# A Strassen MLP whose norms move into the output projection, with a PSUM bank of its own for each product and no elementwise work on GpSimd

## The chip, the cores and the metric

The kernel runs on one core of a Trainium2 chip. The metric is the device time of one execution in microseconds (us). Five engines work side by side, each through its own queue in order: TensorE (PE, matmuls and transposes), VectorE (DVE), ScalarE (ACT), GpSimd (POOL) and SyncE (SP), whose queue issues nearly all DMA transfers. Matmul results land in PSUM, which has eight banks of 512 fp32 values per partition; everything else on the chip lies in SBUF.

## The reference

One residual layer over x of 1024 tokens by 1024 channels, in fp32. An attention and pooling mixer (two branches, gated and merged) ends in an output projection, and an MLP follows:

```
merged = gates_pool * (y_pool @ w_branch_pool) + gates_attn * (y_attn @ w_branch_attn)
x  = x + merged @ w_out                       # output projection, residual
h2 = rmsnorm(x, g_ffn)                        # over the 1024 channels of a token
x  = x + square(relu(h2 @ w_up)) @ w_down     # w_up 1024 x 4096, w_down 4096 x 1024
```

## The kernel before

**Three matmuls for one.** To keep fp32 accuracy each operand is split into a high part (an ACT cast to the rounded type, line 109) and a low part (operand minus high part, line 110, on DVE or POOL). `mm3` (lines 115 to 117) issues high x high, high x low and low x high into the same bank. A split is therefore one ACT and one DVE or POOL instruction per operand tile.

**The stages.** Attention, pooling and gates come first, then the branch projections (`ba`) and the output projection: `out_proj` writes bank `op`, one half of the channels (`dh`) of one block of 128 tokens (t = 0 to 7) at a time, with 24 matmuls each. DVE adds the residual (line 813) and the row goes to DRAM (`yd`). The order is token half th and channel half dh: (0,0), (0,1), (1,1), (1,0), so tokens 0 to 3 are complete half-way and token 7 at the very end.

**The norms.** `norm_token` loads each token block back from DRAM (`yt`), squares and sums on ACT, takes the power -0.5 on POOL (line 235), scales on DVE (line 891, tile `hn`), and transposes on PE into the banks `hb` (line 895).

**The Strassen products.** Both MLP matmuls use the seven-product scheme of Strassen (in Winograd's form), once. The tokens' side of the up projection needs the quarters B11, B21 (tokens 0 to 3), B22 and the combinations T1 to T4 (tokens 0 to 3 with 4 to 7), each split in high and low. Products 1 and 2 need only B11 and B21. A pair p (0 to 15) is 256 columns of w_up: `up_pair` loads them (`wu`), makes the sums S1 to S4 (tiles `s`), splits them (`A`, `AS`), and runs seven products of 12 matmuls. Product 1 goes to bank X, product 2 to Y; 6 and 7 add to X, product 5 and then product 3 go to Z, product 4 to W. `finish` adds a saved partial result (DVE, line 855), applies relu (ACT, line 968) and squares (POOL, line 969). The results and four combinations of them (tiles `us`, DVE) go to DRAM as the operands of the down projection, which runs its seven products (banks DX, DY, DZ, DV) in 8 steps q of 24 matmuls, each with a 0.5 MB load of `ur`, one or two of `wd`, two splits (`u` and `w`) and mostly one difference (T).

**What sets the order.** The program is written in order, with the first part of pair p+1 (products 1 and 2) before the rest of pair p, and the scheduler of the framework sorts each engine's queue by its own time estimates, with the written order as priority. From then on each engine works its queue strictly in that order. Tiles come from pools with a number of buffers; a new tile waits until its buffer's last reader is done. The eight banks of PSUM go round: `bank(name)` takes the next.

## Time and profile before

| | us |
|---|---|
| median of 3 runs (lowest, highest) | 1636.32 (1632.89, 1637.15) |
| profiled execution: its time | 1636.88 |
| profiled execution: span, first to last instruction | 1635.1 |
| busy PE / DVE / ACT / POOL | 1557.7 / 966.0 / 766.2 / 736.6 |
| first matmul of the output projection | 842.2 |
| its last matmul starts | 929.05 |
| first up product starts | 974.08 |
| last down product's last matmul starts | 1631.08 |

PE counts as busy from a matmul's start to its modelled end, so a stage with PE at 100% has matmuls at full spacing. "Granted clock" is the share of full speed that the clock control gave to PE. In a row of groups stand busy us, the mean ns of one, then the idle time of the engine just before these instructions and what ended it.

### The profile page before, as it was taken

What the parts mean: (1) busy time and instruction counts of PE and PEld (TensorE: products, weight loads), DVE (VectorE), ACT (ScalarE), POOL (GpSimd) and SP (SyncE); (2) the same over time, 40 slices, a digit from 0 to 9 for tenths busy, and PEclk for the clock granted to TensorE, in tenths of its full rate; (3) what the DMA queues carried; (4) which work ended last, traced back from release to release, by engine and by line L of the source; (5) the groups of instructions that cost most, each with busy time, mean ns of one, the idle gap of its engine ahead of it and who ended that gap; (6) DMA issues with size and microseconds to landing.
All of it is one profiled execution on the core that took longest, in us unless ns stands there. A gap on an engine that the chain in (4) does not pass through costs nothing.

```text
span 1635.1 us, 22296 instructions
## 1 busy us (share of the span) xinstructions
PE 1557.7 (95%) x7649; PEld 1334.0 (82%) x7649; DVE 966.0 (59%) x2089; ACT 766.2 (47%) x1712; POOL 736.6 (45%) x691
## 2 busy tenths in 40 slices
PE   7999999999999999999999748999999999899999
PEld 6999999999999898887888636887777778688887
DVE  6776767777878787552321176655555474534453
ACT  6656565656665556544311164444434433333332
POOL 5424242425252523125532149876666554345443
PEclk9999999999999999999999959999999999999999
DMA  7112121202021212376342234444333378736763
GB/s 218 59 43 68 37 78 34 72 22 85 31 76 35 78 46 69 107 258 204 120 167 103 89 117 140 144 135 142 135 142 142 142 265 294 244 118 203 271 210 105
DMA packets 147707, 206.43 MB, mean 126 GB/s; under 512 B 9781, under 2 KB 86282, under 8 KB 147594
## 3 DMA queue, kind: packets, MB, share of 16 engines
q1 hardware_dynamic: 137098, 190.29, 35.0%
q10 hardware_dynamic: 10496, 14.72, 2.5%
q8 instruction: 60, 0.98, 0.3%
q14 instruction: 53, 0.43, 0.1%
HBM read 152.51 MB, written 52.46 MB: 125 GB/s over the span
## 4 chain that ended last, share of the span: by engine, by line
PE 80%; DVE 8%; DMA 5%; POOL 3%; issue 2%; ACT 2%; SPq 0%; ACTq 0%; POOLq 0%; DVEq 0%
PE z L117 5%; PE z L115 5%; PE z L116 5%; PE g L115 3%; PE g L116 3%; PE g L117 3%; PE DX L117 3%; PE DX L116 3%; PE DX L115 2%; PE X L115 2%; PE sc L485 2%; PE sc L486 2%; PE X L116 2%; PE X L117 2%; PE Z L115 2%
## 5 line engine op out<-in xcount | busy, mean ns | idle before, releaser
L115 PE MATMUL z<-wqkv,hT 128*128 128x384 f32 x512 | 175.0, 342 | 0.3 <-DVE qn L427 0.2
L117 PE MATMUL z<-wqkv,hT 128*128 128x384 f32 x512 | 174.6, 341 | 0.5 <-DVE hT L110 0.5
L116 PE MATMUL z<-wqkv,hT 128*128 128x384 f32 x512 | 174.1, 340 | 0.0
L235 POOL TENSOR_TENSOR ms<-ms,mhalf 128x4 f32<-128x4 f32 x64 | 66.6, 1041 | 159.1 <-DVE ms L234 140.0
L496 ACT ACTIVATE s<-s,nm 128x256 f32<-128x256 f32 (+7 forms) x128 | 99.6, 778 | 49.4 <-DVE nm L488 45.8
L116 PE MATMUL g<-hT,fwgate 128*128 128x512 f32 x256 | 101.0, 394 | 0.0
L117 PE MATMUL g<-hT,fwgate 128*128 128x512 f32 x256 | 101.0, 394 | 0.0
L115 PE MATMUL g<-hT,fwgate 128*128 128x512 f32 x256 | 100.9, 395 | 0.0
L115 PEld LDWEIGHTS z<-wqkv,hT 128*128 128x128 f32 x512 | 96.9, 189 | 4.2 <-DVE qn L427 0.8
L117 PEld LDWEIGHTS z<-wqkv,hT 128*128 128x128 f32 x512 | 96.9, 189 | 3.2 <-DVE hT L110 1.3
L116 PEld LDWEIGHTS z<-wqkv,hT 128*128 128x128 f32 x512 | 97.0, 189 | 3.0
L433 POOL TENSOR_TENSOR qn<-qn,ggh 128x128 f32<-128x128 f32 x64 | 32.4, 507 | 137.6 <-DVE qn L427 131.4
L969 POOL TENSOR_TENSOR u<-u 128x512 f32<-128x512 f32 x64 | 72.9, 1139 | 43.1 <-ACT u L968 43.1
L488 DVE CUSTOM_DVE_ANT_0 s<-sc,dist 128x512 f32<-128x512 f32 (+3 forms) x128 | 74.7, 586 | 22.3 <-PE sc L486 20.7
L110 POOL TENSOR_TENSOR wqkv<-rqkv,wqkv 128x384 fp32r<-128x384 f32 x60 | 63.3, 1073 | 20.0 <-ACT wqkv L109 18.2
L968 ACT ACTIVATE u<-u 128x512 f32<-128x512 f32 x64 | 40.4, 632 | 65.4 <-DVE u L855 65.0
L110 POOL TENSOR_TENSOR fwgate<-frgate,fwgate 128x512 fp32r<-128x512 f32 x32 | 45.0, 1408 | 53.3 <-ACT fwgate L109 53.2
L485 PE MATMUL sc<-K,Q 128*128 128x512 f32 (+2 forms) x192 | 67.4, 356 | 0.1
L486 PE MATMUL sc<-K,Q 128*128 128x512 f32 (+2 forms) x192 | 66.6, 354 | 0.0
L109 ACT CAST AS<-s 128x512 fp32r<-128x512 f32 x64 | 39.5, 620 | 55.6 <-PE X L117 19.9
L110 DVE TENSOR_TENSOR AS<-s,AS 128x512 fp32r<-128x512 f32 x32 | 37.1, 1160 | 45.4 <-ACT AS L109 45.1
L459 ACT CAST Q<-tk 64x128 fp32r<-64x128 f32 x128 | 33.3, 260 | 58.4 <-DVE Q L458 56.5
(525 smaller groups left out, 4903.9 us busy)
## 6 DMA issues: line engine op xcount, KB each, us to landing
wd<-in_w_down_dram SPq DMA_DIRECT2D x64, 512.0 KB, 4.5
wu<-in_w_up_dram SPq DMA_DIRECT2D x32, 512.0 KB, 3.8
udS<-us SPq DMA_DIRECT2D x64, 256.0 KB, 2.1
ur<-udS SPq DMA_DIRECT2D x32, 512.0 KB, 4.0
rqkv<-in_w_in_dram SPq DMA_DIRECT2D x64, 192.0 KB, 2.8
ud<-u SPq DMA_DIRECT2D x48, 256.0 KB, 2.5
ur<-ud SPq DMA_DIRECT2D x24, 512.0 KB, 4.3
frgate<-in_w_gate_dram SPq DMA_DIRECT2D x32, 256.0 KB, 2.7
```

The source lines that it names most:

```text
L109: nc.scalar.copy(hi, src)
L110: (lo_eng or nc.vector).tensor_tensor(lo, src, f(hi), op=ALU.subtract)
L115: nc.tensor.matmul(ps, lhs_hi, rhs_hi, start=first, stop=False, **kw)
L116: nc.tensor.matmul(ps, lhs_hi, rhs_lo, start=False, stop=False, **kw)
L117: nc.tensor.matmul(ps, lhs_lo, rhs_hi, start=False, stop=last, **kw)
L235: nc.gpsimd.tensor_tensor(dst, dst, mhalf[:, :n], op=ALU.pow)
L485: nc.tensor.matmul(dst, Q[:, i, 0, :], rhs, start=True, stop=False)
L486: nc.tensor.matmul(dst, Q[:, i, 1, :], rhs, start=False, stop=True)
L488: nc.vector.tensor_tensor_reduce(out=s[i][:, c : c + w], in0=sc[:, 0:w], in1=dist[:, o0 + c : o0 + c + w], scale=2.0 ** -(h + 1), scalar=B ...
L496: nc.scalar.activation(s[i][:, 0:n], s[i][:, 0:n], AF.Exp, bias=last, scale=-1.0, accum_out=Z[:, i, t : t + 1])
L968: nc.scalar.activation(r, r, AF.Relu)
L969: pool.tensor_tensor(r, r, r, op=ALU.mult)
```

## The change

The projection's norms, the pools of the MLP, the engines of the elementwise work and the order of the first pairs are rewritten. What is computed and the number of matmuls and transposes stay the same.

- **Norms inside the projection.** A token block stays in SBUF (`py`, four buffers) instead of being loaded back. `first_half` normalises tokens 0 to 3 behind the (1,1) blocks of the projection and writes what the combinations need of them to DRAM (`nd`); `second_half` normalises tokens 4 to 7 with the priority of the (1,0) blocks and makes T1, T2; `combine` makes T3, B22 and T4 later. ACT now scales by the root (a Copy with a scale), DVE multiplies by the gain, once for each half.
- **Four pairs ahead.** Products 1 and 2 of pairs 0 to 3 are written before the rest of pair 0; the second half of a pair's columns (A21, A22) is loaded later, by a transfer of its own. After that it is again one pair ahead.
- **Banks.** X has four banks, Y two, Z and W one each, by name. In the down projection there are two groups of four.
- **No elementwise work on POOL.** Low splits and S sums go to DVE, the squares to ACT. POOL keeps the power in the norms and the splits of `w_out`.
- **Other.** Weights and activations of the down projection get buffers of their own, its first three steps' operands are made early, and the difference T1 (`t1_made`) is made two steps behind. The finished quarters are stored through ACT's queue.

Up to the projection's (1,1) blocks the order of PE is the same instruction for instruction.

PE between the projection and product 6 of pair 0, before (`op` is the projection, `hb` the transposes of token blocks 0 to 7, the first digit behind X, Y or Z the pair; first matmul of each group):

```order
L117 MATMUL op7_0_10140<-wo10_6_1_10056,mT7_1_9620 128x512
L895 MATMUL hb0_0_10202<-identf_81,hn0_10195 128x128 x4
L895 MATMUL hb7_1_10464<-identf_81,hn7_10451 128x128 x4
L115 MATMUL X0_10551<-B11h_10215,A11_0_10553 128x512
L115 MATMUL Y0_10552<-B21h_10223,A12_0_10570 128x512
L115 MATMUL X1_10594<-B11h_10215,A11_1_10596 128x512
L115 MATMUL Y1_10595<-B21h_10223,A12_1_10613 128x512
L115 MATMUL X0_10551<-BT2h_10342,AS2_0_10639 128x512
```

and now, from the last matmul of the projection:

```order
L119 MATMUL op7_0_10292<-wo10_6_1_10204,mT7_1_9626 128x512
L117 MATMUL X0_10533<-B11h_9644,A11_0_10535 128x512
L117 MATMUL Y0_10534<-B21h_9646,A12_0_10552 128x512
L117 MATMUL X1_10598<-B11h_9644,A11_1_10600 128x512
L888 MATMUL hb5_0_10452<-identf_87,y5_10001 128x128 x4
L117 MATMUL X3_10696<-B11h_9644,A11_3_10698 128x512
L888 MATMUL hb7_1_10518<-identf_87,y7_10117 128x128 x4
L117 MATMUL Y2_10648<-B21h_9646,A12_2_10666 128x512
L117 MATMUL Y3_10697<-B21h_9646,A12_3_10715 128x512
L117 MATMUL X0_10533<-BT2h_10345,AS2_0_10751 128x512
L117 MATMUL Z0_10768<-BT1h_10347,AS1_0_10769 128x512
L119 MATMUL X0_10533<-BT2h_10345,AS2_0_10751 128x512
```

All 64 transposes stood alone behind the projection. Now the first 40 stand inside it, and the last 24 between the eight products (96 matmuls) that need only B11 and B21.

DVE in the same place now, from the add that completes token block 7 (entry 1 of this count) to the low halves of S2 and S1 of pair 0 (entries 55 and 56); shown are entries 1, 5, 10, 29, 36, 43, 49, 50, 51, 55 and 56:

```order
L823 TENSOR_TENSOR y7_10117<-op7_0_10292,y7_10117 128x512
L826 TENSOR_TENSOR t1_4_10411<-hb4_0_10422,t1_4_10411 128x512
L884 TENSOR_TENSOR y7_10117<-y7_10117,gfb_9648 128x512 x2
L826 TENSOR_TENSOR t1_7_10501<-hb7_0_10512,t1_7_10501 128x512
L112 TENSOR_TENSOR BT2l_10346<-t2_7_10502,BT2h_10345 128x4x128
L826 TENSOR_TENSOR t4_7_10593<-t4_7_10593,y7_10117 128x512
L823 TENSOR_TENSOR u11_3_10730<-Y3_10697,x1_3_10713 128x512
L823 TENSOR_TENSOR s1_0_10745<-wu0_1_10743 128x512
L826 TENSOR_TENSOR s2_0_10746<-s1_0_10745,wu0_0_10531 128x512
L112 TENSOR_TENSOR AS2_0_10751<-s2_0_10746,AS2_0_10751 128x512
L112 TENSOR_TENSOR AS1_0_10769<-s1_0_10745,AS1_0_10769 128x512
```

Before, this work was shared by DVE and POOL; now it is one queue, and all combinations of tokens 4 to 7 stand ahead of the first S sum.

PE in the steady state, before (first matmul of each product; the products in this order are 3, 4, 1, 2, 5):

```order
L115 MATMUL Z6_11616<-B22h_10355,AS4_6_11658 128x512
L115 MATMUL W7_11846<-BT4h_10361,A22_7_11847 128x512
L115 MATMUL X9_11874<-B11h_10215,A11_9_11876 128x512
L115 MATMUL Y9_11875<-B21h_10223,A12_9_11893 128x512
L115 MATMUL Z8_11936<-BT1h_10346,AS1_8_11937 128x512
```

and now (the last matmul of product 3 of pair 7, then the beginnings of what follows):

```order
L119 MATMUL Z7_11808<-B22h_10351,AS4_7_11850 128x512
L119 MATMUL X8_11744<-BT2h_10345,AS2_8_11951 128x512
L117 MATMUL X11_12224<-B11h_9644,A11_11_12226 128x512
L117 MATMUL Y10_12065<-B21h_9646,A12_10_12083 128x512
L117 MATMUL Z8_11968<-BT1h_10347,AS1_8_11969 128x512
L117 MATMUL W8_12038<-BT4h_10353,A22_8_12039 128x512
```

Between the end of product 3 of a pair and product 5 of the next, which now use the same bank, stand 18 matmuls: the last four of X8, twelve of X11 and two of Y10.

The diff, cut to what the prediction speaks of:

```diff
-N_OP, N_RW, N_SM, N_EV = 8, 8, 4, 9
+N_OP, N_E1, N_E2, N_R1, N_R2 = 8, 11, 6, 4, 3
...
+    nb_pool = pool_of(hs, "nb", 4, side="right")
+    pr1 = pool_of(hs, "pr1", N_R1, side="right")
+    py = pool_of(norms, "py", 4, side="right")
...
     def out_proj(ws, t, dh):
...
+        if t not in y:
+            y[t] = py.tile([P, D], F32, tag="y", name=f"y{t}")
+        nc.sync.dma_start(y[t][:, cs], x[t * P : (t + 1) * P, cs])
...
+    def norm_token(t, bank_fn):
...
+        nc.scalar.activation(sq, yn, AF.Square, accum_out=ss)
+        rsq(rs, ss, 1, 1.0 / D)
+        nc.scalar.activation(yn, yn, AF.Copy, scale=rs)
+        ps = []
+        for j in range(2):
+            js = slice(j * 512, (j + 1) * 512)
+            nc.vector.tensor_tensor(yn[:, js], yn[:, js], gfb[:, js], op=ALU.mult)
+            b = bank_fn(j, f"hb{t}_{j}")
...
+    def first_half(t):
+        b11, b21 = norm_token(t, lambda j, name: bank(name))
+        b_split("11", t * P, b11, dve)
+        b_split("21", t * P, b21, dve)
...
+        nc.sync.dma_start(nd[0, t], r11)
+        nc.sync.dma_start(nd[1, t], d21)
...
             out_proj(ws, t, dh)
+            if (th, dh) == (1, 1):
+                first_half(t - 4)
+            prio[t] = tc.cur_priority
...
+    bm = pool_of(mlp_ps, "bm", 1, PSUM)
+    bx = pool_of(mlp_ps, "bx", 1, PSUM)
...
+    def second_half(t):
+        c0 = (t - 4) * P
+        t1, t2 = (ev(f"{n}_{t}", (P, 4, P)) for n in ("t1", "t2"))
+        nc.sync.dma_start(t1, nd[0, t - 4])
+        b12, b22 = norm_token(t, lambda j, name: bm.tile([P, 512], F32, tag="ZW"[j], name=name))
+        sub(dve, t1, b12, t1)
+        sub(dve, t2, b22, t1)
...
+        b_split("T2", c0, t2, dve)
+        b_split("T1", c0, t1, dve)
...
-        X, Y = bank(f"X{p}"), bank(f"Y{p}")
+        A = load(0, pr1)
+        X = bx.tile([P, 512], F32, tag="X", name=f"X{p}", bufs=4)
+        Y = (bm if p % 2 else bx).tile([P, 512], F32, tag="Y", name=f"Y{p}")
...
-            pool.tensor_tensor(r, r, r, op=ALU.mult)
+            nc.scalar.activation(r, r, AF.Square)
...
-        add(pool, S1, A["21"], A["22"])
-        sub(pool, S2, S1, A["11"])
+        add(dve, S1, A["21"], A["22"])
+        sub(dve, S2, S1, A["11"])
...
-        Z = bank(f"Z{p}")
-        u_product(Z, "5", a_op(p, "S1", S1, pool))
+        Z = bm.tile([P, 512], F32, tag="Z", name=f"Z{p}")
+        u_product(Z, "5", a_op(p, "S1", S1, dve))
...
+    AHEAD = 4
+    for p, q in zip(range(AHEAD), ("T3", "22", "T4", "")):
+        next(pairs[p])
...
+        if q:
+            combine(q)
...
+    pur = pool_of(ctx, "pur", 3, side="right")
+    puo = pool_of(ctx, "puo", 8, side="right")
+    prw = pool_of(ctx, "prw", 7, side="right")
+    pwo = pool_of(ctx, "pwo", 8)
...
-        for n, src, eng in (("u", ur, dve), ("w", second(j, q), pool)):
-            hi, lo = (op([P, 2, 512], f"{n}{j}_{q}{x}") for x in "hl")
-            split(hi, lo, src, eng)
+        for n, src, pool_ in (("u", ur, puo), ("w", second(j, q), pwo)):
+            hi, lo = (pool_.tile([P, 2, 512], F32R, tag="op", name=f"{n}{j}_{q}{x}") for x in "hl")
+            split(hi, lo, src, dve)
...
+    def d_product(banks, j, last=False, early={}):
         for q in range(NQ - 2 if last else NQ):
-            d_step(banks, j, q, operands(j, q), range(4))
+            d_step(banks, j, q, early.get(q) or operands(j, q), range(4))
+            if j == "1" and q > 1:
+                t1_made(q - 2)
...
+    early = {q: operands("1", q) for q in range(3)}
```

More of the change, by code (lines that the diff above doesn't have):

```diff
@@ L773, in encoder_kernel @@
     ws_bp = load_cols2(w_branch_pool, 0, "bp0")
-    ypT = [load_split(p_dram, g * P, f"ypT{g}", htile) for g in range(4)]
+    ypT = [load_split(p_dram, g * P, f"ypT{g}", ypt_tile) for g in range(4)]
     mp, yT = [], []
@@ L820, in w_out_half, with b_split @@
         return ws
+    def b_split(q, c0, src, eng):
+        hi, lo = Bq[q]
+        split(hi[:, :, c0 : c0 + P], lo[:, :, c0 : c0 + P], src, eng)
+    def norm_token(t, bank_fn):
+        ss = const.tile([P, 1], F32, tag="nss", name=f"nss{t}", bufs=2)
+        rs = const.tile([P, 1], F32, tag="nrs", name=f"nrs{t}", bufs=2)
+        sq = nt.tile([P, D], F32, tag="sq", name=f"nsq{t}")
+        yn = y[t]
+        nc.scalar.activation(sq, yn, AF.Square, accum_out=ss)
[6 more added lines that the diff above has]
+            b = bank_fn(j, f"hb{t}_{j}")
+            for i in range(4):
+                k = 4 * j + i
+                nc.tensor.transpose(b[:, i * P : (i + 1) * P], yn[:, k * P : (k + 1) * P], identf)
+            ps.append(b.rearrange("p (a b) -> p a b", a=4))
+        return ps
+    nd = dram.tile([2, 4, P, 4, P], F32, name="nd")
+    def first_half(t):
+        b11, b21 = norm_token(t, lambda j, name: bank(name))
+        b_split("11", t * P, b11, dve)
+        b_split("21", t * P, b21, dve)
+        r11, d21 = (tmp(f"{n}_{t}").rearrange("p (a b) -> p a b", a=4) for n in ("r11", "d21"))
+        nc.scalar.copy(r11, b11)
+        sub(dve, d21, b21, r11)
+        nc.sync.dma_start(nd[0, t], r11)
+        nc.sync.dma_start(nd[1, t], d21)
+    prio = {}
     for th, dh in ((0, 0), (0, 1), (1, 1), (1, 0)):
@@ L920, in encoder_kernel, with ev @@
-    for t in range(NT):
-        norm_token(t)
+    hpT = pool_of(hs, "hpT", 10)
+    pw = pool_of(hs, "pw", N_OP - 2)
+    e1 = pool_of(hs, "e1", N_E1)
+    pw1 = pool_of(hs, "pw1", 2)
+    mlp_ps = ctx.enter_context(ExitStack())
+    bm = pool_of(mlp_ps, "bm", 1, PSUM)
+    bx = pool_of(mlp_ps, "bx", 1, PSUM)
+    def ev(name, shape=(P, 512)):
+        return e1.tile(list(shape), F32, tag="ev", name=name)
+    for q in ("T2", "T1", "T3", "22", "T4"):
+        Bq[q] = tuple(hpT.tile([P, 4, 512], F32R, tag="h", name=f"B{q}{i}") for i in "hl")
@@ new lines, in combine @@
+    def combine(q):
+        for t in range(4, NT):
+            c0 = (t - 4) * P
+            t3, b22 = kept_b[t][:, 0], kept_b[t][:, 1]
+            if q == "T3":
+                sub(dve, t3, b22, t3)
+                b_split(q, c0, t3, dve)
+                T4s[t] = ev(f"t4_{t}", (P, 4, P))
+                nc.sync.dma_start(T4s[t], nd[1, t - 4])
+                sub(dve, T4s[t], T4s[t], t3)
+            elif q == "22":
+                b_split(q, c0, b22, dve)
+            else:
+                b_split(q, c0, T4s[t], dve)
@@ L1006, in up_pair @@
         store("S3", s3)
-        W = bank(f"W{p}")
+        W = bm.tile([P, 512], F32, tag="W", name=f"W{p}")
         u_product(W, "4", a_op(p, "22", A["22"], dve))
         finish("21", W, U3)
-        store("12", C["21"])
+        store("12", C["21"], nc.scalar)
         s4 = ev(f"us4_{p}")
@@ L1015, in encoder_kernel @@
     pairs = [up_pair(p) for p in range(NP)]
-    next(pairs[0])
+    now = tc.cur_priority
+    for t in range(4, NT):
+        tc.cur_priority = prio[min(t + 1, NT - 1)]
+        second_half(t)
+    tc.cur_priority = now
+    AHEAD = 4
+    for p, q in zip(range(AHEAD), ("T3", "22", "T4", "")):
+        next(pairs[p])
+        if q == "T4":
+            body = tc.cur_priority
+        if q:
+            combine(q)
+    norms.close()
+    e2 = pool_of(hs, "e2", N_E2, side="right")
+    pr2 = pool_of(hs, "pr2", N_R2, side="right")
+    now, tc.cur_priority = tc.cur_priority, body
+    for _ in pairs[0]:
+        pass
+    tc.cur_priority = now
     for p in range(NP):
+        if p == NP - 1:
+            last_pair = tc.cur_priority
         if p + 1 < NP:
+            if p + 1 >= AHEAD:
+                next(pairs[p + 1])
             next(pairs[p + 1])
@@ L1114, in finish_out, with four @@
             nc.sync.dma_start(out[r0 : r0 + P, dh * 512 : (dh + 1) * 512], parts[t])
-    def four(name):
-        return [bank(f"{name}{t}") for t in range(4)]
-    DX = four("DX")
-    d_product(DX, "1")
+    def four(tag):
+        return [bd.tile([P, 512], F32, tag=tag, name=f"D{tag}{t}", bufs=4) for t in range(4)]
+    now, tc.cur_priority = tc.cur_priority, last_pair
+    early = {q: operands("1", q) for q in range(3)}
+    tc.cur_priority = now
+    DX = four("a")
+    d_product(DX, "1", early=early)
     x1 = with_residual(DX, "x1y", 0, 0)
-    DY = four("DY")
+    DY = four("b")
     d_product(DY, "2")
```

217 lines of the change are left out of this document (92 added, 125 removed).

## The prediction

> **What bounds the kernel now.** I read the busy time by stage first, to see where TensorE (PE) is not issuing. Columns: stage, length, busy us and (count) of PE, weight loads, DVE, ACT, POOL, then granted PE clock, DMA share, GB/s.
>
> ```profile
> 842.00:929.30 87.30, 87.30 (x386) 72.06 (x384) 11.76 (x17) 8.51 (x14) 17.70 (x14) 1.00 0.29 103
> 929.30:974.00 44.70, 15.70 (x64) 12.25 (x64) 29.29 (x49) 25.36 (x54) 13.43 (x14) 0.56 0.35 118
> 974.00:1007.00 33.00, 26.16 (x96) 19.93 (x96) 21.70 (x27) 16.76 (x30) 28.84 (x21) 0.88 0.51 160
> 1007.00:1100.00 93.00, 93.00 (x402) 75.40 (x401) 56.47 (x54) 38.90 (x69) 74.59 (x55) 1.00 0.42 141
> 1100.00:1300.00 200.00, 187.55 (x799) 149.58 (x798) 109.08 (x117) 82.26 (x143) 122.00 (x101) 1.00 0.40 141
> 1300.00:1345.00 45.00, 40.93 (x168) 32.04 (x167) 30.02 (x23) 16.80 (x22) 25.82 (x13) 0.96 0.64 222
> 1345.00:1405.00 60.00, 60.00 (x266) 49.70 (x265) 33.09 (x23) 22.05 (x22) 28.03 (x11) 1.00 0.81 290
> 1405.00:1424.00 19.00, 13.64 (x52) 10.51 (x51) 13.32 (x11) 3.99 (x4) 5.19 (x3) 0.91 0.84 275
> 1424.00:1631.40 207.40, 207.40 (x916) 171.44 (x914) 90.43 (x76) 74.17 (x74) 95.43 (x37) 1.00 0.54 181
> ```
>
> In the output projection (842 to 929) PE is full and DVE and ACT are nearly empty. Then come the norms, 44.7 us with 15.7 us of PE at a clock of 0.56. The up projection is full to 1100, has holes to 1300, and the down projection has two holes (1300 to 1345, 1405 to 1424). The waits of PE from 870 us on name them:
>
> ```profile
> PE hb L895 <- DVE hn L891: 24.5, 8, 6.4
> PE Z L115 <- DVE u L855: 12.5, 9, 1.4
> PE X L115 <- ACT AS L109: 6.1, 1, 6.1
> PE DX L117 <- DVE u_1l L110: 4.4, 1, 4.4
> ```
>
> So everything before 842 is bound by PE and not touched, and behind 929.3 PE is bound by elementwise work. To turn this into a sum I need what PE must do at the least. The spacing of matmuls where PE waits for nothing, in the up products (1036.05 and 1038.83 are 12 apart) and in the last down product (six apart):
>
> ```profile
> 1036.05 0.40 PE L115 MATMUL X<-BT2h,AS 128*128 128x512 f32 x1
> 1038.83 0.40 PE L115 MATMUL Z<-BT1h,AS 128*128 128x512 f32 x1
> 1629.72 0.39 PE L116 MATMUL DV<-w_7l,u_7h 128*128 128x512 f32 x1
> 1631.08 0.39 PE L117 MATMUL DV<-w_7h,u_7l 128*128 128x512 f32 x1
> 679.82 0.82 PE L541 MATMUL ta<-identf,s 128*128 128x128 f32 x6
> 680.39 0.48 PE L117 MATMUL g<-hT,fwgate 128*128 128x512 f32 x1
> ```
>
> That is 0.232 us in the up part and 0.2267 us in the down part, and about 0.10 us for a transpose at full clock (six in 0.57 us). Each part has 16 x 7 x 12 = 1344 matmuls (the loops), so 312 and 305 us, and 64 transposes need 7 us: 624 us. The last matmul starts at 1631.08, so from 929.3 to 1631.3 they take 702 us. **78 us are stall or half clock**: about 38 around the norms, 11 to 1007, 14 in the up part's holes, 15 in the down part.
>
> **The change part by part.**
>
> *GpSimd's work goes to DVE and ACT.* How dear is it there? DVE's groups between 1007 and 1290, with POOL busy, then the same forms between 1290 and 1300, where POOL has mostly stopped, and their starts:
>
> ```profile
> L110 DVE TENSOR_TENSOR AS<-s,AS 128x512 fp32r<-128x512 f32 x29 | 33.6, 1159 | 38.7 <-ACT AS L109 38.5
> L855 DVE TENSOR_TENSOR us<-u,u 128x512 f32<-128x512 f32 x13 | 23.0, 1770 | 26.0 <-POOL u L969 26.0
> L858 DVE TENSOR_TENSOR us<-us,u 128x512 f32<-128x512 f32 x13 | 21.7, 1667 | 0.4
> L855 DVE TENSOR_TENSOR u<-Z,U 128x512 f32<-128x512 f32 x13 | 9.0, 692 | 18.6 <-PE Z L117 18.6
> ...
> L858 DVE TENSOR_TENSOR us<-us,u 128x512 f32<-128x512 f32 x1 | 0.7, 693 | 0.0
> L855 DVE TENSOR_TENSOR us<-u,u 128x512 f32<-128x512 f32 x1 | 0.7, 691 | 1.2 <-POOL u L969 1.2
> ...
> 1292.58 0.69 DVE L855 TENSOR_TENSOR us<-u,u 128x512 f32<-128x512 f32 x1 [1.23 <-POOL u L969]
> 1293.31 0.69 DVE L858 TENSOR_TENSOR us<-us,u 128x512 f32<-128x512 f32 x1
> 1293.91 0.69 DVE L858 TENSOR_TENSOR us<-u,u 128x512 f32<-128x512 f32 x1
> 1294.52 0.69 DVE L855 TENSOR_TENSOR u<-W,U 128x512 f32<-128x512 f32 x1
> ```
>
> A DVE operation on 128x512 from two SBUF tiles takes 0.9 to 1.8 us beside POOL and 0.69 us alone; one that reads a PSUM bank takes 0.69 us either way. Alone they start 0.61 us apart, 0.73 where one reads the other's result. The Trainium skill (SBUF — State Buffer, section "Who interferes with whom") says the same as a rule: a DVE instruction with two SBUF inputs contends with a GpSimd instruction that reads SBUF, one with a single SBUF input does not. By that rule all of DVE's operations behind the projection should run at 0.69 us; the trace agrees, 692 ns for u<-Z,U with POOL busy.
>
> DVE now has 19 such operations for each pair of columns (seven low splits, four S sums of the weights, four adds of `finish`, four combinations `us`), 19 x 0.64 = 12.2 us against 84 x 0.232 = 19.5 us of PE. ACT, whose rows are
>
> ```profile
> 1110.39 0.58 ACT L961 COPY x<-X 128x512 f32<-128x512 f32 x1
> 1110.87 0.59 ACT L983 COPY U<-X 128x512 f32<-128x512 f32 x1
> L968 ACT ACTIVATE u<-u 128x512 f32<-128x512 f32 x64 | 40.4, 632 | 65.4 <-DVE u L855 65.0
> ```
>
> has seven high casts, four copies, four relus and now four squares: 19 at 0.48 to 0.63 us, 9 to 12 us, and three DMA issues. Both fit beside PE, so the squares and sums cost nothing while PE is the bound; were that cover gone, they would cost 12.2 us a pair.
>
> *Own banks.* The holes between 1100 and 1300 come once a pair:
>
> ```profile
> 1107.62 0.39 PE L117 MATMUL Y<-B21h,A 128*128 128x512 f32 x1
> 1128.76 0.39 PE L117 MATMUL Y<-B21h,A 128*128 128x512 f32 x1
> 1130.54 0.47 PE L115 MATMUL Z<-BT1h,AS 128*128 128x512 f32 x1 [1.38 <-DVE u L855]
> ```
>
> A pair takes 21.14 us, and PE waits 1.38 us for an add that DVE makes late, because DVE stands behind POOL's squares and slow sums. With DVE at 12.2 us that add comes early. The new danger is that Z has a single bank: product 5 of a pair waits until `finish` has read product 3 of the pair before. In the new order 18 matmuls (4.2 us) lie between them, and the add needs one DVE slot of 0.69 us. I take no wait here in the steady state; the bound above is today's 1.4 us for each of 16 pairs, 22 us.
>
> *Norms inside the projection.* 40 transposes (4 us) move into it; for the first four tokens DVE has about six operations (4 us) and ACT about five (4 us) per 5.4 us of PE: hidden under those 87 us, in which DVE is now busy for 11.8. The reload of y (yt<-yd) goes away. For the last four tokens not all can be hidden. After the last projection matmul (call it T0) PE has products 1 and 2 of four pairs and six groups of transposes, 96 x 0.232 + 24 x 0.10 = 24.7 us, and then needs the low half of S2 for product 6 of pair 0. In DVE's new order it is the 55th entry from the add that waits for T0 on (that one counted): 55 slots of 0.61 us, some ten of them dependent (0.12 more) and about 1 us of waits for ACT's scaling of the last token, 36 us. **So PE stands still for about 11.5 us.** Bounds: if ACT and DVE got a third of it done earlier, nothing; at 0.69 us a slot and 5 us of waits between DVE, ACT and PE, 43 - 25 = 18 us. I take the count, since DVE is in order and its durations are measured. Behind it DVE gains on PE again (at pair 2 it is some 7 us ahead by the same count).
>
> *The clock.* A gap of 6.5 us at 987 was followed by this:
>
> ```profile
> 987.00:993.60 6.60, 0.62 (x3) 0.18 (x1) 3.16 (x4) 2.58 (x6) 6.60 (x6) 0.91 0.71 238
> 993.60:999.20 5.60, 5.51 (x13) 4.35 (x14) 3.05 (x3) 3.00 (x7) 5.60 (x5) 0.50 0.47 143
> ```
>
> 5.6 us at half clock, 2.8 us lost. I add 2.7 us. The Trainium skill (TensorE: Matmul & The Clock Gate, section "Why this matters for your kernels") speaks against leaving such a gap: one of more than some 3 us sends TensorE back to half rate. By its warm-up of about 3.4 us the loss would be 1.7 us (an estimate); the rows have more.
>
> *End of the up part.* With pairs 14 and 15 alone in flight, product 5 stands directly behind product 3 of the pair before on the one Z bank, twice: semaphore and one add, 1 us each. The first down product needs the low half of its weights, which DVE makes behind the last `finish`: 0.69 + 1.2 us, 2 us. Together 4 us; bounds 2 and 8.
>
> *Down part.* For each of the 56 steps of 24 matmuls (5.44 us) DVE has two splits and mostly one difference, now all alone:
>
> ```profile
> L858 DVE TENSOR_TENSOR T<-wd,wd 128x1024 f32<-128x1024 f32 x8 | 18.3, 2317 | 0.0
> L858 DVE TENSOR_TENSOR wd<-wd,wd 128x1024 f32<-128x1024 f32 x8 | 10.0, 1250 | 20.2 <-DMA wd<-in_w_down_dram 20.2
> L110 DVE TENSOR_TENSOR u_0l<-ur,u_0h 128x1024 fp32r<-128x1024 f32 x6 | 7.3, 1224 | 14.0 <-ACT u_0h L109 14.0
> ```
>
> 3 x 1.23 = 3.7 us, which fits, and the T1 differences now come behind the splits that PE waits for. What stays is the DMA: product 1 runs at 290 GB/s with a share of 0.81 (stage 1345 to 1405), and the new order asks for the quarters of product 7 before product 6 begins, on SP's one queue. About 26 loads of 0.5 MB in 50 us are 270 GB/s, just inside that. I take 3 us; bounds 0 and the 15 us that this part loses now.
>
> **The sum.** 929.3 + 7 + 312 + 305 = 1553.3, plus the tail from the last matmul's end to the span's end (1635.1 - 1631.3 = 3.8): 1557.1 with no loss at all. Plus 11.5 + 2.7 + 4 + 3 = 21.2: span 1578.3. The profiled execution took 1636.9 for its span of 1635.1, so 1.8 more: **1580 us**. It lies 0.6 us above the median of 1636.32, which I neglect.
>
> **The rivals.**
>
> *The gap is hidden:* DVE and ACT do enough before T0, or their slots overlap better. For it: both stand idle most of the projection. Against: the count above, and that tokens 4 to 7 are complete only in the projection's last 22 us. Time: 1580 - 14 = 1566.
>
> *The single Z bank costs what the shared banks cost:* for it, that wait is the one of today, and DVE holds its queue for ACT (38.7 us idle at AS now). Against: 4.2 us of cover. 16 x 1.4 = 22: 1602.
>
> *DMA becomes the bound in the down part* at the quarters of products 6 and 7: the hole at 1407 to 1419 is such a place today (SP, then DVE late). Another 8 to 12 us: about 1590.
>
> *DVE becomes the bound, and the kernel slower than before.* If the 1.16 us of AS<-s,AS were DVE's own and not POOL's doing, a pair would need 19 x 1.16 = 22.0 us, 2.5 more than PE, 40 us over 16 pairs; the gap behind T0 would be 55 x 1.16 - 25 = 39, 27 more; and three operations of 1.8 us and more on 32 down steps some 17: about 1664. It decides from a mean of 1.03 us (19.5 / 19) upwards in the up part. The rows of 0.69 us stand against it.
>
> *Nothing gained:* the new waits eat the 78 us (1636). I see no mechanism of that size besides the last.
>
> **How the numbers follow.** 1580 as worked out, with its own range of 1571 to 1589: 0.46. Hidden gap, 1566: 0.18. Z bank, 1602: 0.14. DMA, 1590: 0.13. DVE bound: 0.04. Nothing gained within 0.3% (5 us, about what a measurement of this kernel can tell from no change): 0.02. The rest, 0.03, lies between 1605 and 1630. The range of 1563 to 1604 leaves out the last three and part of the first's sides. Faster 0.94, same 0.02, slower 0.04.
>
> **What would show it.** Right: no gap of PE over 1 us between 842 and T0 (about 933); one gap of 8 to 15 us with a wait for DVE's low split of AS (line 112) some 25 us later, and 3 to 7 us of half clock; then pairs 19.5 us apart with DVE's SBUF operations at 0.69 us; PE full in the down part but for 3 to 7 us. Wrong: pairs at 21 us or more (Z bank); DVE at over 1 us without POOL; PE in the down part waiting for splits whose idle time ends with wd or ur loads; or a gap behind T0 under 5 us.

## The result and the profile after

The changed kernel takes **1582.3 us** (median of 4 runs, 1580.79 to 1589.36) against 1636.74 us of the kernel before (1632.89 to 1637.28 on the same chip): a ratio of **0.9681, 95% interval 0.9648 to 0.9713**. Repeated later beside other kernels it had 1583.15 us (5 runs), ratio 0.9685 (0.9671 to 0.9699). The prediction was 1580 us.

The profiled execution is the slowest of the four: 1589.36 us, span 1587.6. Its busy time by stage, with the columns of the first table of the prediction:

```profile
842.00:933.80 91.80, 91.80 (x427) 76.45 (x426) 30.57 (x52) 32.42 (x50) 21.51 (x21) 1.00 0.50 163
933.80:953.00 19.20, 19.20 (x96) 15.66 (x95) 17.18 (x29) 14.26 (x26) 0.55 (x1) 1.00 0.48 152
953.00:980.00 27.00, 19.81 (x68) 15.22 (x67) 25.80 (x44) 19.03 (x35) 0.00 (x0) 0.81 0.48 139
980.00:1231.00 251.00, 251.00 (x1098) 205.53 (x1097) 160.48 (x247) 142.50 (x244) 0.00 (x0) 1.00 0.44 147
1231.00:1276.00 45.00, 36.14 (x139) 26.99 (x138) 25.50 (x35) 23.23 (x37) 0.00 (x0) 0.92 0.66 235
1276.00:1310.00 34.00, 34.00 (x147) 27.55 (x146) 21.56 (x19) 12.49 (x13) 0.00 (x0) 1.00 1.03 377
1430.00:1550.00 120.00, 120.00 (x516) 97.21 (x515) 71.71 (x69) 41.95 (x42) 0.00 (x0) 1.00 0.65 208
```

Compare it with the stages before. The projection is still full, now with the transposes of five token blocks in it. The 77.7 us from 929.3 to 1007 that had 41.86 us of PE have become one loss between 953 and 980. From 980 to 1231 PE is full: 1098 matmuls at 251 / 1098 = 0.2286 us, so a pair of 84 takes 19.2 us, not 21.14. A second loss lies between 1231 and 1276. Behind it PE is full to the end. PE's waits from 870 us on:

```profile
PE Z L117 <- DVE u L823: 4.5, 2, 3.7
PE Y L117 <- DVE u L823: 3.6, 1, 3.6
PE X L117 <- ACT AS L111: 3.6, 1, 3.6
PE Da L117 <- DVE u L823: 1.5, 1, 1.5
PE W L117 <- DVE u L823: 1.0, 1, 1.0
```

The two behind the projection, in order of time (the bracket is PE's idle time before the matmul and what ended it):

```profile
956.92 0.79 PE L117 MATMUL Y<-B21h,A 128*128 128x512 f32 x1 [3.60 <-DVE u L823]
967.91 0.79 PE L117 MATMUL X<-BT2h,AS 128*128 128x512 f32 x1 [3.59 <-ACT AS L111]
```

The waits of 24.5 us for `hn` and of 12.5 us for Z are gone. What is left behind the projection is 3.6 us for a Y bank and 3.6 us for S2 of pair 0.

One thing has no place in these waits. From 1430 to 1550 PE issues 516 matmuls in 120 us, 0.2326 us each; before it was 0.2267 us in the down part. In the up part it went the other way: 0.2324 us before, 0.2267 to 0.2288 us now for products 3 to 7. PE waits for nothing in either. That was the first question for the experiments.

### The profile page after: what moved, and what is told of

Its sections match the earlier page's. It is cut to its first block, busy times and chain, and to the rows that moved or that the text cites. A ratio compares the mean times of both kernels' runs of the same rounds, so it can differ in the third digit from the quotient of the medians.

```text
span 1587.6 us, 21976 instructions
## 1 busy us (share of the span) xinstructions
PE 1551.9 (98%) x7649; PEld 1328.8 (84%) x7649; DVE 1008.6 (64%) x2265; ACT 812.1 (51%) x1776; POOL 347.8 (22%) x447
## 4 chain that ended last, share of the span: by engine, by line
PE 88%; DVE 4%; DMA 4%; ACT 1%; issue 1%; POOL 1%; SPq 1%; ACTq 0%; DVEq 0%; POOLq 0%
PE z L117 5%; PE z L119 5%; PE z L118 5%; PE Da L117 4%; PE Da L118 4%; PE Da L119 4%; PE g L118 3%; PE g L117 3%; PE g L119 3%; PE Db L118 3%; PE Db L119 3%; PE Db L117 3%; PE X L117 3%; PE X L118 3%; PE X L119 3%; PE sc L490 2%
## 5 line engine op out<-in xcount | busy, mean ns | idle before, releaser
L112 POOL TENSOR_TENSOR wqkv<-rqkv,wqkv 128x384 fp32r<-128x384 f32 x60 | 63.2, 1071 | 20.2 <-ACT wqkv L111 19.2
L112 DVE TENSOR_TENSOR AS<-s,AS 128x512 fp32r<-128x512 f32 x64 | 43.7, 689 | 31.4 <-ACT AS L111 31.4
L464 ACT CAST Q<-tk 64x128 fp32r<-64x128 f32 x128 | 33.2, 259 | 58.7 <-DVE Q L463 56.8
L461 ACT CAST Q<-tk 64x128 fp32r<-64x128 f32 x128 | 33.0, 258 | 50.7 <-DVE K L460 49.2
L119 PEld LDWEIGHTS g<-hT,fwgate 128*128 128x128 f32 x256 | 48.1, 188 | 8.6
```

The costliest lines, as they stand in the source:

```text
L112: (lo_eng or nc.vector).tensor_tensor(lo, src, f(hi), op=ALU.subtract)
L119: nc.tensor.matmul(ps, lhs_lo, rhs_hi, start=False, stop=last, **kw)
L461: nc.scalar.copy(q_hi, q)
L464: nc.scalar.copy(Q[other, m, 1, :], q)
```

## The experiments

Times are medians; before had 1635.0, 1635.5 and 1635.0 us in the three groups of runs, so they can be compared as they stand. The changed kernel is at 1583.15 us (0.9685).

**Do the addresses of the tiles set the spacing of the matmuls?** In the build the moving tile of the up products before starts at 32, the stationary one at 416 (start address in the partition modulo 512 bytes); in the down part both are at 416. Now products 3 to 7 have 32 and 32, the down part 32 and 480. The first kernel moves tiles by unused bytes so that all are at 32:

```diff
+    fp.tile([P, 96], F32, name="padl")
     attn = mix.enter_context(ExitStack())
...
+    pool_of(ctx, "padr", 1, side="right").tile([P, 112], F32, name="padr")
     hs = ctx.enter_context(ExitStack())
```

> Same instructions in the same order as the changed kernel (1582.3 us); two unused spaces of 448 and 384 bytes per partition only shift where later tiles lie in SBUF. In the trace of the changed kernel matmuls on 512 columns start 0.2267 us apart where the moving and the stationary tile have the same start address modulo 512 bytes (32 and 32: output projection, products 5, 6, 7, 3, 4 of the up part) and 0.233 us apart where they differ (480 and 32: products 1 and 2; 32 and 480: the whole down part; 160 and 32: the branch projection). Here all are at 32. Theory (the addresses set the pitch): 0.0066 us less for each of 1344 + 384 + 384 matmuls, 8.9 + 2.5 + 2.5 = 13.9 us; with waits that absorb some of it, 10 to 14 us less: 1568 to 1572, and the last down product at 0.2267 us. Rival (the pitch follows what DVE, ACT and the DMA engines do beside PE, which is unchanged): no difference, 1579 to 1586, down part still at 0.2324 to 0.233 us.

Measured: **1576.01 us** (1575.37 to 1579.17), ratio 0.9643 (0.963 to 0.9656). The stage 1430 to 1550, aligned:

```profile
1430.00:1550.00 120.00, 120.00 (x531) 99.34 (x530) 74.00 (x71) 44.39 (x45) 0.00 (x0) 1.00 0.59 195
```

531 matmuls in place of 516: 0.226 us. The theory holds and the rival falls, since DVE, ACT and the DMA engines do the same as before. The gain of 7 us is less than the 10 to 14 expected, and the repeat of the changed kernel shows why:

> The changed kernel itself, again, beside the next three. Its first profiled execution (1589.36 us) had the down part at 0.2333 us a matmul, the profiles of two variants with the same addresses had 0.2289 us. Theory (where moving and stationary tile differ in their start address the pitch takes one of two values in an execution): most executions at 1579 to 1583, and the down part at 0.2289 us in the profile unless that execution takes 6 us longer (1344 x 0.0044 = 5.9). Rival (early loads of the down part's operands make the spread, by late adds at the end of the up part): the long executions have the longer stretch 1231 to 1276 and the pitch stays at one value.

```profile
1430.00:1550.00 120.00, 120.00 (x526) 98.47 (x525) 72.83 (x71) 43.35 (x44) 0.00 (x0) 1.00 0.63 204
```

This execution (1581.78 us) had 526 matmuls there: 0.2281 us (0.2289 us for a matmul followed in the same product), not 0.2326. Same program, same addresses. Six more profiles of kernels with this placement, below, also had 0.2289 us. So against the usual execution the alignment is worth 1344 x 0.0022 + 768 x 0.0066 = 8 us, which fits the 7 measured. The first profile was the exception: its 0.2333 us cost 5.9 us more, and that is most of its 7.6 us of additional span. The rival (late adds make the spread) has about 1 us of it: between 1200 and 1300 the starts of the matmuls lost 14 us there and 13 us here. The other executions have no profile, so what their spacing was is not known.

**Which distances matter?** Eight distances between moving and stationary tile in one kernel, the aligned one, one distance for each step q of the down part:

```diff
+            o = (0, 8, 16, 32, 48, 64, 96, 112)[q] if n == "w" else 0   # words of 4 bytes
-                pool_.tile([P, 2, 512], F32R, tag="op", ...)
+                pool_.tile([P, 1024 + 128 * (n == "w")], F32R, tag="op", ...)[:, o : o + 1024]
```

> As the kernel with aligned tiles, but in the down part the moving tiles (w) of steps q = 0 to 7 start 0, 32, 64, 128, 192, 256, 384 and 448 bytes behind the stationary ones modulo 512. Same instructions, same order. Theory (addresses): two groups of steps, some at 0.2267 us between matmuls and some at 0.233 us; step 0 is at 0.2267. If only equality counts, the seven others are slow; if a smaller block counts, the offsets that are multiples of it are fast too (of 128 bytes: 128, 256, 384; of 256 bytes: 256 alone). The cases in hand, 64 and 128 bytes (both slow), speak for 256 or 512. Rival (not the addresses): all eight steps alike. The time lies between those of the aligned and the changed kernel.

1583.25 us (one run). The first matmul of each step of product 5, in order of time:

```profile
1400.07 0.40 PE L118 MATMUL Db<-w_0h,u_0h 128*128 128x512 f32 x1
1405.53 0.40 PE L118 MATMUL Db<-w_1h,u_1h 128*128 128x512 f32 x1
1411.13 0.40 PE L118 MATMUL Db<-w_2h,u_2h 128*128 128x512 f32 x1
1416.64 0.39 PE L118 MATMUL Db<-w_3h,u_3h 128*128 128x512 f32 x1
1422.21 0.39 PE L118 MATMUL Db<-w_4h,u_4h 128*128 128x512 f32 x1
1427.81 0.39 PE L118 MATMUL Db<-w_5h,u_5h 128*128 128x512 f32 x1
1433.27 0.40 PE L118 MATMUL Db<-w_6h,u_6h 128*128 128x512 f32 x1
1438.86 0.39 PE L118 MATMUL Db<-w_7h,u_7h 128*128 128x512 f32 x1
1444.46 0.40 PE L118 MATMUL Da<-w_0h,u_0h 128*128 128x512 f32 x1
```

Each difference divided by 24 matmuls:

| bytes that w starts behind u, modulo 512 | 0 | 32 | 64 | 128 | 192 | 256 | 384 | 448 |
|---|---|---|---|---|---|---|---|---|
| us for a matmul | 0.2275 | 0.2333 | 0.2296 | 0.2321 | 0.2333 | 0.2275 | 0.2329 | 0.2333 |

The other full products have the same values within 0.0003, with DMA shares between 0.48 and 0.97 beside them. (The edge of a step is in these figures: at distance 0 matmuls of one product follow each other after 0.2267 us.) So 0 and 256 are alike and fast, 64 is between, the rest is slow. The up part before (32 and 416, a distance of 128) had 0.2324; products 1 and 2 now (448) 0.2333; the down part now (64) 0.2289, once 0.2333.

**The same in the kernel before**, 384 unused bytes ahead of the tokens' operands:

```diff
+    hs.enter_context(tc.tile_pool(name="padh", bufs=1)).tile([P, 96], F32, name="padh")
     hp = hs.enter_context(tc.tile_pool(name="hp", bufs=14, reuse_waits="tile"))
```

> The kernel before, same instructions and order, with 384 unused bytes ahead of the tokens' operands, so that moving and stationary tile of all up products start at the same address modulo 512 bytes (416 and 416 in place of 32 and 416). Theory (addresses set the pitch, in any kernel): the up products go from 0.2324 to 0.2267 us; where PE is full, to 1100 and in part behind it, 1344 x 0.0057 = 7.7 us less at most, 5 to 7.7 us: 1628 to 1630. Rival (the slow up part is the traffic of GpSimd and DVE): no change, 1634 to 1637.

1630.92 us (10 runs), ratio 0.9975 (0.9965 to 0.9985): 4 us less. Up products where PE is full:

```profile
1007.00:1100.00 93.00, 93.00 (x412) 1.00 0.43 144
```

412 matmuls against 402. The spacing fell in full, to 0.2267 us, but the time fell by less than the 5 to 7.7 us expected. Where the pair waits for its add, part of the gain became wait (13.6 us for Z in place of 12.5); in the profile the first down product starts 5.6 us earlier (1295.4 against 1301.0). In the down part this execution, the slowest of the ten, lost 2 us of that again: it had 13.7 us at half clock there in place of 6.8.

**GpSimd put back in the up part.**

```diff
-            nc.scalar.activation(r, r, AF.Square)
+            pool.tensor_tensor(r, r, r, op=ALU.mult)
...
-        add(dve, S1, A["21"], A["22"])
+        add(pool, S1, A["21"], A["22"])        # S2, S3, S4 and the low halves of A12, AS1, AS4 likewise
```

> The changed kernel with one part undone: in the up part GpSimd again makes the four squares, the four S sums and the low halves of A12, AS1 and AS4 of each pair, as before; the banks, the norms and the down part stay as changed. Theory (GpSimd's work is what cost the pair): DVE's operations with two SBUF inputs take 0.9 to 1.8 us again where POOL is busy, the pair goes from 19.1 to 20 to 21 us: 15 to 30 us slower than the changed kernel, 1597 to 1612. Rival (the shared PSUM banks cost the pair, and these have gone): pairs stay within 0.2 us of 19.1, 1580 to 1586.

**1599.8 us** (1597.68 to 1603.16), ratio 0.9785 (0.9771 to 0.9799). The time is the theory's, the reason only in part. DVE's groups between 1050 and 1200:

```profile
L112 DVE TENSOR_TENSOR AS<-s,AS 128x512 fp32r<-128x512 f32 x16 | 19.6, 1224 | 15.5 <-ACT AS L111 15.3
L826 DVE TENSOR_TENSOR us<-us,u 128x512 f32<-128x512 f32 x8 | 5.5, 692 | 0.3
```

The stages of this kernel:

```profile
953.00:980.00 27.00, 18.96 (x61) 14.93 (x62) 19.11 (x25) 14.32 (x26) 20.04 (x14) 0.75 0.38 117
980.00:1007.00 27.00, 20.53 (x83) 16.41 (x82) 14.55 (x13) 8.59 (x15) 24.46 (x18) 0.90 0.41 127
1050.00:1200.00 150.00, 150.00 (x656) 122.78 (x655) 72.22 (x94) 69.20 (x118) 106.29 (x86) 1.00 0.43 147
```

The low halves of AS take 1224 ns again (691 in the changed kernel); the `us` sums, which no longer fall into GpSimd's work, stay at 692. But the pairs stay full: 656 matmuls in 150 us, as without GpSimd. The 17 us are lost at the start (some 12 us more between 950 and 1050) and at the end of the up part (some 5 us), much of it in waits for the add that frees bank W:

```profile
PE W L117 <- DVE u L823: 13.0, 4, 6.5
```

So the rival is right about the steady pairs: there the new banks and the longer lead together are enough. Which of these two it is was not tried apart.

**No GpSimd in the up part of the kernel before**, its banks and norms as they were:

```diff
-            pool.tensor_tensor(r, r, r, op=ALU.mult)
+            nc.scalar.activation(r, r, AF.Square)
...
-        add(pool, S1, A["21"], A["22"])
+        add(dve, S1, A["21"], A["22"])         # and the rest of the list above
```

> The kernel before with one part of the change alone: in the up part the squares go to ACT and the S sums and the low halves of A12, AS1 and AS4 to DVE; the eight banks still go round, the norms stay alone behind the projection, the down part is as before. The changed kernel with GpSimd put back kept its pairs full, so own banks are enough against the 1.38 us wait of each pair; is GpSimd's absence enough too? Theory of the prediction (that wait is DVE's add, late because DVE stands behind GpSimd's squares and sums): the wait goes without new banks, the pair from 21.14 to 19.5 to 19.8 us, the stretch 1007 to 1300 loses 2 to 4 us in place of 14: 1621 to 1626. Rival (the shared banks make the wait whoever does the elementwise work): pairs stay at 20.5 us or more, 1630 to 1637.

**1617.16 us** (1614.96 to 1619.2), ratio 0.9888 (0.9867 to 0.9909): 18 us less. The stage of the holes:

```profile
1100.00:1300.00 200.00, 200.00 (x862) 162.16 (x861) 119.42 (x179) 109.14 (x187) 2.52 (x2) 1.00 0.42 148
```

DVE's low halves of the sums, between 1007 and 1290:

```profile
L110 DVE TENSOR_TENSOR AS<-s,AS 128x512 fp32r<-128x512 f32 x56 | 38.6, 690 | 44.0 <-ACT AS L109 44.0
```

PE is full with the old, shared banks (187.55 us before), which is worth some 14 us; another 3 us less are lost in the down part, so the time is below the 1621 to 1626 that the theory gave. So either alone closes the holes of the pairs, GpSimd's absence or the banks with the longer lead; in the change they do it twice, and the 14 us there must not be counted for both.

**GpSimd put back in the down part**, for the low halves of w:

```diff
-            split(hi, lo, src, dve)
+            split(hi, lo, src, pool if n == "w" else dve)
```

> The changed kernel with one other part undone: in the down part GpSimd again makes the low halves of the weights (w). Theory (GpSimd at 2.5 us for each and DVE slowed beside it made the 15 us that the down part lost before): holes come back at the start of the down part, where a difference is made as well, and at the change to products 6 and 7: 5 to 15 us more than the changed kernel, 1588 to 1598. Rival (the buffers, two groups of operands, T1 two steps behind, cured it): 0 to 3 us, 1582 to 1586.

1591.0 us (1588.02 to 1593.53), ratio 0.9727 (0.9705 to 0.9748): 8 us more. The loss lies at the first down product alone (PE lost 13.5 us from 1250 to 1300, the changed kernel 7 to 8): the waits there grew and one is new.

```profile
PE Z L117 <- DVE u L823: 4.0, 2, 3.2
PE Da L117 <- DVE u L823: 2.9, 1, 2.9
PE Da L118 <- POOL w_0l L112: 1.9, 1, 1.9
```

The hole at the change to products 6 and 7 (1405 to 1424 in the kernel before, half of its 15 us) does not come back. There the rival is right: buffers and order cured it.

**Two pairs begun ahead in place of four.**

```diff
-    AHEAD = 4
-    for p, q in zip(range(AHEAD), ("T3", "22", "T4", "")):
-        next(pairs[p])
+    AHEAD = 2
+    for p, q in zip(range(4), ("T3", "22", "T4", "")):
+        if p < AHEAD:
+            next(pairs[p])
```

> The changed kernel with two pairs begun ahead in place of four. Behind the projection PE has 72 matmuls and 24 transposes (19 us) in place of 96 (24.7 us) before product 6 of pair 0, and DVE's queue has its low half of S2 at entry 51 in place of 55 (33 us). Theory (the stall there is DVE's queue less PE's cover): 13 to 14 us of stall in place of the 11 to 12 measured, so 1 to 4 us slower, 1583 to 1587; the cover is worth less than its 5.6 us since DVE's work for the two pairs goes too. Rival (the cover counts in full): 5 to 7 us slower, 1588 to 1590. Rival (not the cover but the loads): no change.

1589.09 us (1586.22 to 1595.05), ratio 0.972 (0.9695 to 0.9745): 6 us more. The median lies in the range of the rival that counts the cover in full and just outside the theory's; the interval reaches both. PE's wait behind the projection:

```profile
PE X L117 <- ACT AS L111: 13.4, 1, 13.4
```

It is one wait of 13.4 us in place of two of 3.6, as the count had it (13 to 14). Idle time and half clock together grew by 4.6 us between 950 and 1000 (16.4 in place of 11.8); the theory had set 13 to 14 us of idle time against 11 to 12 that held half clock already. The loads as the sole cause are out.

**The sums of pair 0 ahead of the combinations.**

```diff
+    raw0 = hpT.tile([P, 4, 512], F32, tag="h", name="wu0_1")   # later a half of T4
...
+            raw0[:, 1 + i].rearrange("p (a b) -> p a b", b=P) if p == 0 and i < 3
...
-        if q == "T4":
+        if q == "T3":
             body = tc.cur_priority
```

> The changed kernel, but the second half of pair 0's columns and its sums S1, S2 lie in a buffer that is free early (the one that later holds a half of T4), loaded before the projection ends, and the rest of pair 0 has a priority ahead of the combinations T3, B22 and T4. In DVE's queue the low halves of S2 and S1 move from entries 55 and 56 behind the projection's last add to about entries 25 and 26; what product 6 then needs last is the last low half of T2, entry 41, and product 3 the low half of S4, entry 53. Theory (the stall behind the projection is DVE's queue, entries times 0.61 us, against PE's cover): PE has 8 products, 24 transposes and products 6, 5, 7 (33 us) before it needs entry 53 (35 us); of the 13.1 us lost between 933 and 980 about 4 stay: 9 us less, 1573. Rival (the stall is set by the DMA loads or by ACT's casts): 0 to 2 us less, 1580 to 1583, with the gaps where they were.

1578.89 us (1578.07 to 1580.41), ratio 0.9656 (0.9643 to 0.9669): 4 to 5 us less. PE's waits and the stage behind the projection:

```profile
PE Z L117 <- ACT BT1h L111: 1.9, 1, 1.9
PE X L117 <- ACT BT2h L111: 1.1, 1, 1.1
```

```profile
953.00:980.00 27.00, 23.95 (x94) 18.97 (x94) 26.00 (x44) 21.34 (x41) 0.00 (x0) 0.87 0.38 117
```

PE is busy 23.95 us of the 27 in place of 19.81. S2 is no longer what it waits for, so the order of DVE's queue did set the stall. (The edit also loads the second half of the columns earlier, but in the changed kernel DVE had been busy for 25.80 of these 27 us.) Half of the hoped gain is missing because PE now begins with products 5 and 6 and waits for T1 and T2 of the last token, while Y2 and Y3, which could fill the time, stand behind them.

**Is it the bank at the end of the up part?**

```diff
-        Z = bm.tile([P, 512], F32, tag="Z", name=f"Z{p}")
+        Z = bx.tile([P, 512], F32, tag="X", name=f"Z{p}", bufs=4) if p >= NP - 2 else bm.tile(...)
-        W = bm.tile([P, 512], F32, tag="W", name=f"W{p}")
+        W = bx.tile([P, 512], F32, tag="X", name=f"W{p}", bufs=4) if p >= NP - 1 else bm.tile(...)
```

> The changed kernel, but pairs 14 and 15 take the bank for products 5 and 3, and pair 15 that for product 4, from the four X banks, two of which are no longer used by then. Theory (at the end of the up part the single Z bank makes PE wait for the add behind product 3 of the pair before, which DVE does late, behind the early down operands): the gaps of 4.1, 1.2 and 1.3 us at 1231, 1251 and 1264 and that of 2.2 us at 1270 go, and about 3 us of half clock with them; of the 14 us lost between 1231 and 1276 some 4 to 6 stay: 7 to 9 us less, 1573 to 1575. Rival (PE is held by DVE and ACT there and only waits one product later): 0 to 3 us less, 1579 to 1582, and the same idle time at other places before the first down product.

1584.33 us (1581.3 to 1585.81), ratio 0.9686 (0.9672 to 0.9699): nothing. The theory falls. PE's longest wait there is now another:

```profile
PE X L117 <- ACT U L1026: 4.4, 1, 4.4
```

ACT's queue in order of time (ACTq is a DMA that ACT issues) shows what stands ahead of that copy:

```profile
1257.66 0.63 ACT L1009 ACTIVATE u<-u 128x512 f32<-128x512 f32 x1 [2.69 <-DVE u L823]
1258.32 0.63 ACT L1010 ACTIVATE u<-u 128x512 f32<-128x512 f32 x1
1258.98 0.33 ACTq L1014 DMA_DIRECT2D ud<-u  x1
1259.35 0.59 ACT L1026 COPY U<-X 128x512 f32<-128x512 f32 x1 [0.40 <-ACT u L1010]
```

The copy of X that product 7 of pair 15 needs stands behind relu, square and store of product 4 of pair 14; these wait for an add that stands on DVE behind three `us` sums, which wait for ACT's squares. With two pairs left PE has nothing to run in the meantime.

**So take that chain apart**, for the last two pairs alone (with the banks of the last kernel):

```diff
-            nc.scalar.activation(r, r, AF.Relu)
-            nc.scalar.activation(r, r, AF.Square)
+            if p >= NP - 2:
+                dve.scalar_tensor_tensor(r, r, 0.0, r, op0=ALU.max, op1=ALU.mult)
+            else: ...
-            queue.dma_start(ud[name, p // 2][:, p % 2, :], src)
+            (queue if p < NP - 2 else nc.sync).dma_start(ud[name, p // 2][:, p % 2, :], src)
```

> The changed kernel with three edits for the last two pairs alone: banks for products 5, 3 (and 4 of pair 15) from the X banks as before; relu and square as one DVE operation (maximum with zero, times itself) in place of two on ACT; their stores through SP's queue in place of ACT's. Theory (the end of the up part is a chain of dependent steps with ACT's queue in it: copies of X that PE waits for stand behind relu, square and stores that wait for DVE): the 4.4 us wait for ACT's copy of X that the kernel with the banks alone showed goes, with its half clock; of the 15 us lost between 1200 and 1300 6 to 9 stay: 6 to 9 us less than the changed kernel, 1573 to 1576. Rival (DMA loads of the first down operands, or DVE, hold PE there): the loss stays at 13 to 15 us and the time at 1580 to 1583.

**1575.48 us** (1573.03 to 1576.97), ratio 0.9633 (0.962 to 0.9646): 8 us less, as the theory had it. The stage from 1231 to 1276, and PE's waits there:

```profile
1231.00:1276.00 45.00, 38.30 (x165) 30.32 (x164) 32.66 (x43) 18.27 (x27) 0.00 (x0) 1.00 0.73 258
```

```profile
PE Z L117 <- DVE u L823: 2.7, 1, 2.7
PE Da L118 <- DVE w_0l L112: 2.4, 1, 2.4
PE W L117 <- DVE u L823: 1.6, 1, 1.6
```

165 matmuls in place of 139, and the clock stays at 1.00. Of the 7 us between this profile and that of the repeat, 5 lie between 1225 and 1295 (7.8 us lost in place of 12.8). Some 2 us lie ahead of the projection's end, which the edits don't touch and which moves by up to 3 us from one profile to the next. Which of the three edits does most was not tried apart; the bank alone did nothing.

**Together**: alignment, pair 0's sums and the chain, with the edits shown above.

> Aligned tiles, the early sums of pair 0 and the last pairs' chain together. Theory: the gains add, 6 (aligned) + 3.5 (order) as measured, 6 to 9 for the chain: 1563 to 1567. Rival (the chain is not the cause): 1571 to 1574.

**1563.92 us** (1558.89 to 1566.86), ratio **0.9561 (0.9543 to 0.9578)**. The gains add; this version beats both kernels, the changed one by 19 us.

## Why the prediction was right, point by point

1580 us were predicted, 1582.3 measured, well inside the likeliest case (1571 to 1589). But the total is nearer than its terms, and that part is luck. In the repeat the end of the up part costs 8.6 us more than the sum had and the down matmuls 2.6, against 4.3 less for the up matmuls, 3 less for DMA and 2.4 less for the stall. The terms beside the two profiles of the changed kernel:

| term (us) | predicted | first profile | repeat |
|---|---|---|---|
| end of the projection, 40 transposes in it | 933.3 | 933.8 | 933.8 |
| other 24 transposes, tail | 6.8 | 6.9 | 6.9 |
| up matmuls, 1344 | 312 | 307.7 | 307.7 |
| down matmuls, 1344 | 305 | 313.5 | 307.6 |
| stall and half clock behind the projection | 14.2 | 12.5 | 11.8 |
| end of the up part, to the first down product | 4 | 14 | 12.6 |
| DMA in the down part | 3 | 0 | 0 |
| span | 1578.3 | 1587.6 | 1580.0 |

The matmul rows are counts times the spacings of the trace: 384 x 0.2333 + 960 x 0.2272, and 1344 x 0.2333 or 0.2289. The two rows of loss are what the starts of all matmuls in the trace lie apart beyond that. Each column of measured terms adds up to its span within 1 us.

- **GpSimd's work on DVE and ACT costs nothing in the steady pairs: right.** DVE's low halves of AS take 691 ns (1159 before), PE is full from 980 to 1231, and DVE's 160.48 us there are 12.3 us for each pair (12.2 predicted). The removal of that work from GpSimd alone is worth 18 us in the kernel before.

```profile
L112 DVE TENSOR_TENSOR AS<-s,AS 128x512 fp32r<-128x512 f32 x47 | 32.4, 691 | 27.6 <-ACT AS L111 27.6
```

- **Own banks: right that the 1.38 us go and that the single Z bank costs nothing in the steady state** (no wait for Z between 980 and 1231; that rival, 1602, is out). The reason was only half of it: DVE's lateness and the shared banks are both needed for that wait, and removing either ends it (the banks together with the longer lead).
- **The count of DVE's queue: right.** Its 55th entry was put at 36 us behind the add of entry 1. The trace of the changed kernel has them 35.0 us apart:

```profile
933.94 0.69 DVE L823 TENSOR_TENSOR y<-op,y 128x512 f32<-128x512 f32 x1
...
968.93 1.29 DVE L112 TENSOR_TENSOR AS<-s,AS 128x512 fp32r<-128x512 f32 x2
```

 The form of the stall was wrong. I expected one gap of 11.5 us, and had named a gap under 5 us as a sign of being wrong; there are two of 3.9 us between starts, because Y2 waits for the Y bank of pair 0, whose add is entry 34 of the same queue. The second ends with ACT's cast of S2, not with DVE's low half of it. The first moved idle time forward, and two stretches of half clock took back most of what two short gaps saved: 12.5 us in place of 14.2.
- **The clock: too small by one stretch.** Behind each of the two gaps the starts are 0.43 us apart for a while:

```profile
957.51 0.63 PE L118 MATMUL Y<-B21l,A 128*128 128x512 f32 x1
957.93 0.63 PE L119 MATMUL Y<-B21h,A 128*128 128x512 f32 x1
```

 The granted clock there, in the columns of the stage tables:

```profile
956.90:960.30 3.40, 3.38 (x8) 2.71 (x9) 3.40 (x6) 3.40 (x8) 0.00 (x0) 0.50 0.00 0
967.10:973.90 6.80, 5.99 (x14) 4.52 (x15) 6.80 (x13) 3.95 (x8) 0.00 (x0) 0.50 0.37 116
```

 In the profiles of the changed kernel and of its variants such stretches between 950 and 1300 last 3.41 us, or two or four times that, and within one profile they begin whole multiples of 3.41 us apart (here at 956.88 and 967.12). In the kernel with the chain taken apart a gap of 3.11 us between starts (2.72 idle) cost no half clock: the clock of that stage stayed at 1.00. The Trainium skill (TensorE: Matmul & The Clock Gate, section "Why this matters for your kernels") puts the limit at about 3 us without work; the traces agree only roughly. Behind the projection every gap of 3.4 us of idle time or more had half clock behind it, but the shorter ones went either way. The same wait for `w_0l` at the first down product, 2.42 us in the combined kernel and 2.41 us with the chain taken apart, was followed by this:

```profile
1255.00:1258.40 3.40, 3.29 (x8) 2.61 (x9) 3.40 (x5) 0.44 (x1) 0.00 (x0) 0.50 0.24 93
1261.60:1265.00 3.40, 3.37 (x15) 2.79 (x16) 3.40 (x5) 0.14 (x1) 0.00 (x0) 1.00 0.26 102
```

 The first is the combined kernel, at half clock, the second the other, at full clock. Whether it matters where in such a step of 3.41 us a gap falls, no run here tests. The warm-up of about 3.4 us that the Trainium skill gives (the same page, Part 1) fits the shorter stretch; the longer one is twice as long.
- **End of the up part: the step that failed.** "Semaphore and one add, 1 us each" named the Z bank twice and the first down operands, 4 us, with bounds of 2 and 8. It was 13 to 14 us. The bank is not what holds PE: with banks to spare the loss only moves. With two pairs left the chain PE, DVE's add, ACT's relu and square, DVE's sums, ACT's copy stands open, and ACT's DMA issues, which the change put into that queue, wait in it as well. Costing an edit by its own bank instead of by the queues behind it made it three times too small.
- **DMA in the down part: nothing, at the lower bound.** PE is full from 1276 to 1310 at 377 GB/s and a share of 1.03, and behind it. The rival at 1590 is out.
- **The spacing of the matmuls was taken as fixed for each part**, 0.232 up and 0.2267 down. It belongs to the placement of tiles, which the change swapped. In the usual execution the two differences nearly cancel (4.3 us less up, 2.6 us more down).
- **The hidden gap (1566) is out** by the waits of 3.6 us; **DVE as the bound (1664) and nothing gained** by the 691 ns and the stages.

Where did the 78 us of loss before go? Some 37 of the 49 us around the norms are gone, all 14 of the pairs, and of the 15 us in the down part the hole at products 6 and 7; the loss where the up part runs out has grown from some 7 us (1300 to 1345 before) to 13.

## What to carry to other kernels

Count a stall behind a stage as the entries of the in-order queue that feeds it against the work that the waiting engine still has; the count held to 1 us here. Cost the end of a pipelined loop apart from its steady state: there the dependent chain through every in-order queue counts, DMA issues in it too, and more banks alone did not shorten it here. And where PE is full, look at the spacing of its matmuls before and after: a change of buffers can move it by 2.5% through addresses alone.
